# Attention with an added bias: the second q half loaded behind the bias, the bias slots one place later, and a third late-bias bank

## The chip, the core and the metric

The kernel runs on one core of a Trainium2 chip. Its time is device microseconds of one execution. Seven runs before the change gave a median of 250.71 us, between 250.09 and 253.24 us. One execution was recorded by the hardware profiler; all durations of instructions below come from it.

## The reference

Four batches of eight heads, 1024 positions, 64 values per head. One bias matrix of 1024 by 1024 is shared by all 32 heads.

```python
scores = np.matmul(q, k.transpose(0, 1, 3, 2)) / np.sqrt(64) + bias   # bias [1, 1, 1024, 1024]
attn = np.exp(scores - scores_max) / (np.sum(np.exp(scores - scores_max), axis=-1, keepdims=True) + 1e-8)
out = np.matmul(attn, v)
```

## The kernel before, in words

**Work units.** The heads are taken in 16 pairs. The scores are held transposed: keys on the 128 partitions, 512 queries along the free dimension. Such a block of 128 keys by 512 queries of one head is called a *bank*; there are 512 of them. The banks of a pair run over query half 0 first (16 banks: 8 key chunks by 2 heads) and then over query half 1. So banks 0 to 15 need only the first query half of pair 0, and bank 16 is the first that needs its second half. In the last 16 banks the order is one head after the other.

**Slots.** Banks are grouped into slots, one PSUM buffer and one exp each: slot S0 holds bank 0, S1 banks 1 and 2, and from S2 on each slot has three (S2: 3 to 5, S6: 15 to 17, S7: 18 to 20). The last two are S168 with banks 507 to 509 and S169 with banks 510 and 511. The PSUM pool `ps_s` has two buffers, so a slot can be filled only when the exp of the slot before the last has ended.

**One slot's way.** TensorE fills it (`s_fill`, L130: one matmul of kT with qT a bank). ScalarE takes the exp of it in one instruction (`s_exp`, L137) and writes bf16 to a tile E in SBUF. The bias enters as a factor: exp(score + bias) is exp(score) times exp(bias). VectorE multiplies E by `eb`, the exp of the transposed bias, two or four banks an instruction (`mul_pair`, L156, L159, L162). TensorE then multiplies E by v with a column of ones (`av_bank`, L187; for the last eight banks `av_last`, L223), and VectorE divides by the sum (L197, L199; for the last eight banks L232, L236 and L238) before the output DMA.

**The bias factor.** `eb` is made in four units. In each, 16 TensorE transposes of the raw bias `btraw` go to a PSUM buffer of the same pool `ps_s` (`b_fill`, L145), and one ScalarE exp writes 128x2048 values (`b_exp`, L150). The four units B(0,0), B(0,4), B(1,0), B(1,4) stand at fixed places in the list `order` of slots, L328 to L330.

**Late-bias banks.** For the last banks the bias is added ahead of the exp, as an extra matmul of the identity with `braw` (L133), so that no multiplication comes after the exp. `late_bias` names them (L110): banks 510 and 511. `late_bias_pe` (L164 to L175) makes `braw` from `btraw` by eight transposes and one VectorE instruction with the factor 8 (L174); the piece `(NP, 0, 0)` stands for it in the planner.

**Loads.** k and q of pair 0 come in two halves. The first halves come through the SyncE and ScalarE queues in float32. The second ones, and everything later, are issued by GpSimd with a cast to bf16. At the start GpSimd issues:

```python
nc.gpsimd.dma_start(out=kr0[:, :, QC:, :]..., in_=kf[0][:, :, QC * D:])   # L261: k, second half
nc.gpsimd.dma_start(out=qr0[:, :, QC:, :]..., in_=qf[0][:, :, QC * D:])   # L262: q, second half
nc.gpsimd.dma_start(out=btraw[:, :QC, :], in_=bf_[:, :QC, :])             # L263: bias rows of query half 0
```

After them come v of pair 0 (L81), the other half of the bias (L318), and k, q and v of the next pairs (L75, L76, L81). The second q half of pair 0 is transposed on TensorE (L89) and copied into qT with a mask on VectorE (L98). Then S6 can be filled.

**Order.** Slots S0 to S2 are written out by hand. From S3 on a planner inside the kernel, with costs of its own and due times for the loads (`bias_at`, `raw_at`), decides in which order each engine's instructions are written; each engine then runs its list in order and waits on semaphores. The planner's times decide only this order. Its table `ends` says that the last multiplications take one bank (506), two (507, 508) and one (509); `pe_last` holds banks 508 and 509 together for L223.

Of the kernel before, what the change touches and what calls it, by code (L numbers as in the profile page):

```python
# [15 lines left out]
def kernel(  # L16
# [41 lines left out]
    warm = consts.tile([P, 1], F32)  # L58
    btraw = consts.tile([P, NCH, S], BF)
    eb = consts.tile([P, 2, NCH, HQ], BF)  # L60
    braw = consts.tile([P, 2, HQ], BF)
    mask = consts.tile([P, 2, HQ], BF)
    vall = consts.tile([P, 2 * NP, NCH, D1], BF)

# [18 lines left out]
    def transpose_pe(pr, which, half, tag):  # L83

        src = raws[pr][which]
        px = ps_x.tile([P, QC, P], BF, tag=tag, name="px")
        for c in range(QC):
            for t in range(2):
                nc.tensor.transpose(px[t * D:(t + 1) * D, c, :], src[:, t, half * QC + c, :], ident[:])  # L89
        if (pr, which) not in trs:  # L90
            trs[(pr, which)] = (kvp.tile([P, NCH, P], BF, name="kT") if which else
                                kvp.tile([P, 2, NCH * P], BF, name="qT"))
        dst = trs[(pr, which)]

        def copy():
            if which == 0:

                nc.vector.tensor_tensor(dst[:, :, half * HQ:(half + 1) * HQ],  # L98
                                        px.rearrange("p c q -> p (c q)").unsqueeze(1).to_broadcast([P, 2, HQ]),
                                        mask[:], op=ALU.mult)  # L100
            else:
                nc.vector.tensor_copy(dst[:, half * QC:(half + 1) * QC, :], px[:])  # L102
        return copy
# [3 lines left out]
    NB = len(banks)  # L107

    banks[NB - 16:] = [(NP - 1, h, 1, kc) for h in range(2) for kc in range(NCH)]
    late_bias = {NB - 2: 0, NB - 1: 1}  # L110
    slots = [[0], [1, 2]] + [list(range(i, min(i + 3, NB))) for i in range(3, NB, 3)]
    NS = len(slots)
    ET = 12
# [47 lines left out]
        else:  # L161
            nc.vector.tensor_tensor(e, e, eb[:, qh, kc:kc + 1, :].to_broadcast([P, n, HQ]), op=ALU.mult)  # L162

    def late_bias_pe(tag):  # L164

        px = ps_x.tile([P, 2, HQ], BF, tag=tag, name="px")
        for j in range(2):
            for i in range(QC):
                nc.tensor.transpose(px[:, j, i * P:(i + 1) * P],
                                    btraw[:, QC + i, :].rearrange("p (kp kc) -> p kc kp", kc=NCH)[:, NCH - 2 + j, :],  # L170
                                    ident[:])

        def copy():
            nc.vector.tensor_scalar(braw[:], px[:], 1.0 / scale, None, op0=ALU.mult)  # L174
        return copy  # L175

    oalls = {}
# [64 lines left out]
    with tc.manual_schedule():  # L242
# [16 lines left out]
        nc.gpsimd.memset(qT0[D:, 0, :HQ], 0.0)  # L259
        nc.gpsimd.memset(qT0[:D, 1, :HQ], 0.0)  # L260
        nc.gpsimd.dma_start(out=kr0[:, :, QC:, :].rearrange("p t c d -> p t (c d)"), in_=kf[0][:, :, QC * D:])  # L261
        nc.gpsimd.dma_start(out=qr0[:, :, QC:, :].rearrange("p t c d -> p t (c d)"), in_=qf[0][:, :, QC * D:])  # L262
        nc.gpsimd.dma_start(out=btraw[:, :QC, :], in_=bf_[:, :QC, :])  # L263
        for x in range(2):
            for y in range(2):
                nc.vector.memset(mask[x * D:(x + 1) * D, y, :], 1.0 if x == y else 0.0)
# [59 lines left out]
        EXP, EXP0, QK, AV, TP = 427, 62, 216, 170, 350  # L326
        MUL, COPYQ, COPYK, EVAC, SEM = 600, 650, 420, 620, 80
        order = [("S", g) for g in range(3, NS)]  # L328
        for at, x in ((4, (0, 0)), (6, (0, 4)), (9, (1, 0)), (11, (1, 4))):
            order.insert(at, ("B",) + x)  # L330
        NO = len(order)
        T0 = 8000.0
# [2 lines left out]
        act_end = []  # L335
        x_free = {"xa": T0 - 500, "xb": T0 + 100}
        x_unit = {}
        bias_at = [13300, 20800]
        raw_at = {0: (5900, 7800), 1: (22200, 23500), 2: (26000, 28500)}
        pieces = [(0, 0, 1)]  # L340
        for pr in range(1, NP):
            pieces += [(pr, 1, 0), (pr, 0, 0), (pr, 1, 1), (pr, 0, 1)]

        pieces.append((NP, 0, 0))
        raw_at[NP] = (T0, T0)
        piece_end = {(0, 1, 0): T0, (0, 0, 0): T0, (0, 1, 1): T0 + 200}
        eb_at = {}
# [13 lines left out]
            return banks[b][:3]  # L361

        dve_q = []
        ends = {NB - 6: 1, NB - 5: 2, NB - 3: 1}

        def pe_cost(t, c):
            return c * 2 if t < COLD else c
# [13 lines left out]
        def pe_fill():  # L381
            i = len(filled)
            if i >= NO or i - 2 >= len(act_end):
                return None
            ready = act_end_of(i - 2) + SEM
            item = order[i]
            if item[0] == "S":
                for b in slots[item[1]]:
                    pr, h, qh, kc = banks[b]
                    for key in ((pr, 1, kc // QC), (pr, 0, qh)) + (((NP, 0, 0),) if b in late_bias else ()):  # L390
                        if key not in piece_end:
                            return None
                        ready = max(ready, piece_end[key] + SEM)
                cost = QK * (len(slots[item[1]]) + sum(b in late_bias for b in slots[item[1]]))
            else:
                ready = max(ready, bias_at[item[1]])
                cost = 2 * TP + 250

            def emit(t):
                if item[0] == "S":  # L400
                    s_fill(item[1])
                else:
                    b_fill(item[1], item[2])
                filled.append(t + pe_cost(t, cost))
            return ready, cost, emit

        def pe_piece():
            if not pieces:
                return None
            pr, which, half = pieces[0]  # L410
            if pr not in raw_at or (pr < NP and pr not in raws):
                return None
            i = min(len(filled), NO - 1)
            while order[i][0] != "S":
                i -= 1
            at = slots[order[i][1]][0]
            if at < (pr - 2) * 32 + 8:
                return None

            left = NCH - av_next % NCH  # L420
            busy = x_unit.get(unit_of(av_order[av_next])) if av_next < NA and av_next % NCH else None
            tags = sorted((x_free[x], x) for x in x_free if x != busy)
            if busy and left < 4 and at < pr * 32 - 16:
                return None
            if not busy and av_next and at < pr * 32 - 16 and tags[0][0] + SEM < t_pe and len(tags) > 1 and tags[1][0] > t_pe:
                return None
            free, tag = tags[0]
            ready = max(free + SEM, raw_at[pr][1 - which])
            cost_t = TP if pr < NP else 720

            def emit(t):
                pieces.pop(0)
                copy = transpose_pe(pr, which, half, tag) if pr < NP else late_bias_pe(tag)
                cost = COPYK if which else COPYQ
                x_free[tag] = 1e12

                def run(t2):
                    copy()
                    x_free[tag] = t2 + cost
                    piece_end[(pr, which, half)] = t2 + cost  # L440
                    if pr < NP and which == 0 and half == 1:
                        if pr + 3 < NP:
                            load_qk(pr + 3)
                            raw_at[pr + 3] = (t2 + 7000, t2 + 7000)
                        if pr + 2 < NP:
                            load_v(pr + 2)
                dve_q.append((t + pe_cost(t, cost_t) + SEM, 0, cost, run))
            return ready, cost_t, emit
# [3 lines left out]
        def pe_last():  # L452

            best = None
            for x in range(2):
                left = last_left[x]
                if not left or (x == 1 and last_tag[0] is None):
                    continue
                steps = [[b] for b in left if b not in (NB - 4, NB - 3)] or [[NB - 4, NB - 3]]
                for bs in steps:  # L460
                    if any(b not in mul_at for b in bs):
                        continue
                    ready = max(mul_at[b] for b in bs) + SEM
                    tag = last_tag[x]
                    if tag is None and x == 0:
                        free, tag = min((x_free[y], y) for y in x_free)
                        ready = max(ready, free + SEM)
                    elif tag is None:
                        if len(act_end) < NO - 1 or len(filled) < NO:
                            continue  # L470
                        tag = "s"
                        ready = max(ready, act_end[NO - 2] + SEM)
                    c = (max(ready, t_pe), x, bs, tag)
                    if best is None or c[0] < best[0]:
                        best = c
            if best is None:
                return None
            ready, x, bs, tag = best
            cost = len(bs) * AV // 2

            def emit(t):
                if last_tag[x] is None and x == 0:
                    x_free[tag] = 1e12
                last_tag[x] = tag
                evac = av_last(x, bs, tag)
                if evac:
                    dve_q.append((t + cost + SEM, 1, EVAC, lambda t2: evac()))
            return ready, cost, emit
# [152 lines left out]
```

## Time and profile before

| what | value |
|---|---|
| median of 7 runs | 250.71 us |
| the profiled execution's own time | 250.79 us |
| its span, first to last instruction | 249.0 us |
| ScalarE busy | 239.9 us (96%) |
| TensorE matmul busy | 229.1 us (92%) |
| VectorE busy | 220.7 us (89%) |
| GpSimd busy | 53.6 us (22%) |
| 172 exps of E (L137) | 230.0 us |
| 4 exps of the bias (L150) | 7.5 us |
| ScalarE in the exp of S0 | from 5.87 us |
| last exp of E ends | 243.21 us |

The busy share is read with the idle time of each engine's largest group beside it. The 172 exps have 0.4 us of idle time before them in total, and the four bias exps 0.3 us. The profiled execution's time is its span and 1.8 us around it, and it lies 0.08 us above the median.

### The profile page before, as it was taken

Reading aid. Unit: us, or ns where it says so; the run is one execution under the profiler, and the core shown is the slowest. Engines: PE = TensorE matmul, PEld = TensorE weight load, DVE = VectorE, ACT = ScalarE, POOL = GpSimd, SP = SyncE. Lnnn points to the kernel's source line nnn. Section 1 sums busy time; section 2 is a strip of 40 time slices with the busy share of each in tenths; the row PEclk is TensorE's granted clock in tenths of the full one; section 3 lists DMA queues with packets and bytes.
Section 4 is the critical chain, followed back from the end, with each engine's and each line's share of the span. In section 5 each row is a group of like instructions: output and inputs, shape, how many; then the busy total and the mean of one; then the engine's idle time right before and its main releaser. Section 6 shows DMA issues by size and latency. Waiting matters only on the chain.

```text
span 249.0 us, 7212 instructions
## 1 busy us (share of the span) xinstructions
PE 229.1 (92%) x3160; PEld 140.7 (56%) x3160; DVE 220.7 (89%) x393; ACT 239.9 (96%) x183; POOL 53.6 (22%) x74
## 2 busy tenths in 40 slices
PE   7768999999999999999999999999999999998991
PEld 4346656666555565655655665555565555565561
DVE  5236999999999999999999989999999999998882
ACT  4999999999999999999999999999999999999991
POOL 6653534104013050315050400501600000000000
PEclk9999999999999999999999999999999999999998
DMA  5999999924935649496968921582981111020211
GB/s 122 182 204 188 199 126 206 90 87 54 156 49 92 79 98 116 91 125 85 129 81 120 132 53 42 87 129 42 147 70 42 45 40 48 3 84 3 87 42 46
DMA packets 48464, 23.80 MB, mean 96 GB/s; under 512 B 34480, under 2 KB 44592, under 8 KB 48176
## 3 DMA queue, kind: packets, MB, share of 16 engines
q0 software_dynamic: 42272, 14.42, 53.5%
q1 hardware_dynamic: 5872, 8.72, 9.8%
q8 instruction: 25, 0.41, 0.6%
q10 hardware_dynamic: 288, 0.20, 0.2%
q14 instruction: 7, 0.06, 0.1%
HBM read 29.36 MB, written 8.39 MB: 152 GB/s over the span
## 4 chain that ended last, share of the span: by engine, by line
ACT 57%; PE 20%; DVE 14%; DMA 4%; issue 2%; POOL 1%; ACTq 0%; POOLq 0%
ACT E L137 54%; PE ps L130 12%; DVE E L162 5%; PE po L187 5%; DMA btraw<-in_bias_dram 4%; ACT eb L150 3%; PE px L89 2%; DVE qT L98 2%; DVE E L159 2%; DVE oall L199 2%; DVE E L156 1%; DVE rs L197 1%; DVE kT L102 1%; PE pb L145 0%; POOL kr L261 0%
## 5 line engine op out<-in xcount | busy, mean ns | idle before, releaser
L137 ACT ACTIVATE E<-ps 128x1536 bf16<-128x1536 f32 (+2 forms) x172 | 230.0, 1700 | 0.4 <-PE ps L130 0.4
L130 PE MATMUL ps<-qT,kT 128*128 128x512 bf16 x512 | 138.4, 377 | 8.5 <-ACT E L137 5.3
L187 PEld LDWEIGHTS <-E 128*128 128x128 bf16 x2016 | 81.3, 97 | 40.1 <-DVE E L162 5.1
L187 PE MATMUL po<-vall,E 128*128 128x65 bf16 x2016 | 92.5, 194 | 2.4 <-DVE E L162 1.3
L159 DVE TENSOR_TENSOR E<-E,eb 128x2048 bf16<-128x2048 bf16 x66 | 79.8, 1216 | 6.8 <-ACT eb L150 6.4
L162 DVE TENSOR_TENSOR E<-E,eb 128x1024 bf16<-128x1024 bf16 x116 | 76.6, 683 | 2.7 <-ACT E L137 1.9
L130 PEld LDWEIGHTS <-kT 128*128 128x128 bf16 x512 | 45.2, 96 | 39.7 <-issue 8.4
L75 POOL DMA_DIRECT2D kr<-in_k_dram x15 | 10.5, 700 | 90.8 <-PE px L89 85.2
L81 POOL DMA_DIRECT2D vall<-in_v_dram x32 | 28.1, 883 | 4.9 <-DVE kT L315 3.8
L199 DVE TENSOR_TENSOR oall<-po,rs 128x256 f32<-128x256 f32 x63 | 26.8, 425 | 2.2
L98 DVE TENSOR_TENSOR qT<-px,mask 128x1024 bf16<-128x1024 bf16 x31 | 21.3, 688 | 4.0 <-PE px L89 3.1
L76 POOL DMA_DIRECT2D qr<-in_q_dram x15 | 10.8, 717 | 29.5 <-PE px L89 25.5
L102 DVE COPY kT<-px 128x512 bf16<-128x512 bf16 x30 | 12.6, 421 | 1.8 <-PE px L89 1.2
L197 DVE RECIPROCAL rs<-po 128x4 f32<-128x4 f32 x63 | 11.1, 176 | 2.0 <-PE po L187 1.7
L89 PEld LDWEIGHTS <-qr 128*64 128x64 bf16 x248 | 8.0, 109 | 8.7 <-issue 5.9
L89 PE MATMUL px<-ident,qr 128*64 128x128 bf16 x248 | 12.8, 225 | 0.0
L89 PE MATMUL px<-ident,kr 128*64 128x128 bf16 x240 | 12.4, 224 | 0.1
L89 PEld LDWEIGHTS <-kr 128*64 128x64 bf16 x240 | 7.7, 109 | 7.8 <-issue 3.6
L150 ACT ACTIVATE eb<-pb 128x2048 bf16<-128x2048 bf16 x4 | 7.5, 1877 | 0.3 <-PE pb L145 0.3
L145 PE MATMUL pb<-ident,btraw 128*128 128x128 bf16 x64 | 4.7, 226 | 2.3 <-ACT eb L150 1.5
L145 PEld LDWEIGHTS <-btraw 128*128 128x128 bf16 x64 | 4.4, 147 | 3.2 <-issue 1.6
L156 DVE TENSOR_TENSOR E<-E,eb 128x1024 bf16<-128x1024 bf16 (+2 forms) x7 | 4.6, 686 | 0.2 <-ACT E L137 0.2
(44 smaller groups left out, 27.5 us busy)
## 6 DMA issues: line engine op xcount, KB each, us to landing
out_dram<-oall SPq DMA_DIRECT2D x28, 256.0 KB, 2.0
vall<-in_v_dram POOLq DMA_DIRECT2D x32, 128.0 KB, 5.6
kr<-in_k_dram POOLq DMA_DIRECT2D x15, 256.0 KB, 3.9
qr<-in_q_dram POOLq DMA_DIRECT2D x15, 256.0 KB, 5.1
btraw<-in_bias_dram POOLq DMA_DIRECT2D x2, 1024.0 KB, 9.7
out_dram<-oall SPq DMA_DIRECT2D x7, 128.0 KB, 3.8
k0f<-in_k_dram SPq DMA_DIRECT2D x2, 128.0 KB, 2.9
q0f<-in_q_dram ACTq DMA_DIRECT2D x1, 128.0 KB, 2.7
```

The source lines that it names most:

```text
L81: nc.gpsimd.dma_start(out=vall[:, 2 * pr + t, :, :D], in_=vf[pr, :, t])
L89: nc.tensor.transpose(px[t * D:(t + 1) * D, c, :], src[:, t, half * QC + c, :], ident[:])
L98: nc.vector.tensor_tensor(dst[:, :, half * HQ:(half + 1) * HQ], px.rearrange("p c q -> p (c q)").unsqueeze(1).to_broadcast([P, 2, HQ]), ma ...
L102: nc.vector.tensor_copy(dst[:, half * QC:(half + 1) * QC, :], px[:])
L130: nc.tensor.matmul(ps[:, j, :], kT[:, kc, :], qT[:, h, qh * HQ:(qh + 1) * HQ], start=True, stop=b not in late_bias)
L137: nc.scalar.activation(e_at(slots[g][0], n), open_ps.pop(("S", g))[:, :n, :], ACTF.Exp, scale=scale)
L150: nc.scalar.activation(eb[:, qh, k0:k0 + 4, :], open_ps.pop(("B", qh, k0))[:, :4, :], ACTF.Exp)
L159: nc.vector.tensor_tensor(e, e, eb[:, qh, kc:kc + 2, :].unsqueeze(2).to_broadcast([P, 2, 2, HQ]), op=ALU.mult)
L162: nc.vector.tensor_tensor(e, e, eb[:, qh, kc:kc + 1, :].to_broadcast([P, n, HQ]), op=ALU.mult)
L187: nc.tensor.matmul(acc[:, i, :], e[:, 0, i * P:(i + 1) * P], vall[:, 2 * pr + h, kc, :], start=(kc == 0 and i == 0), stop=(kc == NCH - 1), ...
L197: nc.vector.reciprocal(rs[:], acc[:, :, D:D1])
L199: nc.vector.tensor_tensor(oall[:, c0:c0 + QC, :], acc[:, :, :D], rs[:].to_broadcast([P, QC, D]), op=ALU.mult)
```

## The change

- The load of the second q half of pair 0 is issued behind the load of the first half of the bias instead of ahead of it. The planner's due times follow: the bias at 12.9 us (before 13.3) and 20.2 us (before 20.8), this q half at 13.7 us (before 7.8).
- The four bias units stand one slot later in `order`. The exps run S2 to S7, B(0,0), S8, B(0,4), S9, S10, B(1,0), S11, B(1,4); before they ran S2 to S6, B(0,0), S7, B(0,4), S8, S9, B(1,0), S10, B(1,4).
- Three banks take the bias ahead of the exp: 509, 510 and 511. `braw` has three parts, made in two pieces: one of two banks and one of one bank. Bank 509 has no multiplication after the exp any more, and `pe_last` takes 508 and 509 singly.

From the added line in `late_bias_pe` on, line numbers are one higher after the change.

```diff
-    braw = consts.tile([P, 2, HQ], BF)
+    braw = consts.tile([P, 3, HQ], BF)
...
-    late_bias = {NB - 2: 0, NB - 1: 1}
+    late_bias = {NB - 3 + i: i for i in range(3)}
...
-    def late_bias_pe(tag):
-
-        px = ps_x.tile([P, 2, HQ], BF, tag=tag, name="px")
-        for j in range(2):
+    def late_bias_pe(j0, tag):
+
+        n = min(2, 3 - j0)
+        px = ps_x.tile([P, n, HQ], BF, tag=tag, name="px")
+        for j in range(n):
             for i in range(QC):
                 nc.tensor.transpose(px[:, j, i * P:(i + 1) * P],
-                                    btraw[:, QC + i, :].rearrange("p (kp kc) -> p kc kp", kc=NCH)[:, NCH - 2 + j, :],
+                                    btraw[:, QC + i, :].rearrange("p (kp kc) -> p kc kp", kc=NCH)[:, NCH - 3 + j0 + j, :],
                                     ident[:])
         def copy():
-            nc.vector.tensor_scalar(braw[:], px[:], 1.0 / scale, None, op0=ALU.mult)
+            nc.vector.tensor_scalar(braw[:, j0:j0 + n, :], px[:], 1.0 / scale, None, op0=ALU.mult)
...
         nc.gpsimd.dma_start(out=kr0[:, :, QC:, :].rearrange("p t c d -> p t (c d)"), in_=kf[0][:, :, QC * D:])
+        nc.gpsimd.dma_start(out=btraw[:, :QC, :], in_=bf_[:, :QC, :])
         nc.gpsimd.dma_start(out=qr0[:, :, QC:, :].rearrange("p t c d -> p t (c d)"), in_=qf[0][:, :, QC * D:])
-        nc.gpsimd.dma_start(out=btraw[:, :QC, :], in_=bf_[:, :QC, :])
...
-        for at, x in ((4, (0, 0)), (6, (0, 4)), (9, (1, 0)), (11, (1, 4))):
+        for at, x in ((5, (0, 0)), (7, (0, 4)), (10, (1, 0)), (12, (1, 4))):
             order.insert(at, ("B",) + x)
...
-        bias_at = [13300, 20800]
-        raw_at = {0: (5900, 7800), 1: (22200, 23500), 2: (26000, 28500)}
+        bias_at = [12900, 20200]
+        raw_at = {0: (5900, 13700), 1: (22200, 23500), 2: (26000, 28500)}
...
-        pieces.append((NP, 0, 0))
+        pieces += [(NP, 0, j) for j in range(2)]
...
-        ends = {NB - 6: 1, NB - 5: 2, NB - 3: 1}
+        ends = {NB - 6: 1, NB - 5: 2}
...
-                steps = [[b] for b in left if b not in (NB - 4, NB - 3)] or [[NB - 4, NB - 3]]
+                steps = [[b] for b in left]
```

## The prediction

> **What bounds the kernel now.** I read the page's busy table and costliest groups first.
>
> ```profile
> PE 229.1 (92%) x3160; PEld 140.7 (56%) x3160; DVE 220.7 (89%) x393; ACT 239.9 (96%) x183; POOL 53.6 (22%) x74
> ...
> L137 ACT ACTIVATE E<-ps 128x1536 bf16<-128x1536 f32 (+2 forms) x172 | 230.0, 1700 | 0.4 <-PE ps L130 0.4
> ...
> L150 ACT ACTIVATE eb<-pb 128x2048 bf16<-128x2048 bf16 x4 | 7.5, 1877 | 0.3 <-PE pb L145 0.3
> ```
>
> ScalarE runs 176 exps from 5.87 us to 243.21 us with 0.7 us of idle time before them. Exps of three banks follow each other every 1.34 us (part of the recorded length overlaps the next). So ScalarE is the limit from end to end: a delay in front of any exp is paid in full, and a gain can only come from its small gaps, its start at 5.87 and the tail after 243.21. The other engines can give nothing in between.
>
> Next, the timeline of the first 18 us, start and length first:
>
> ```profile
> 9.87 0.41 PE L89 MATMUL px<-ident,qr 128*64 128x128 bf16 x8
> 10.33 0.69 DVE L98 TENSOR_TENSOR qT<-px,mask 128x1024 bf16<-128x1024 bf16 x1 [1.99 <-PE px L89]
> 11.82 0.81 PE L130 MATMUL ps<-qT,kT 128*128 128x512 bf16 x3 [0.54 <-ACT E L137]
> 12.97 1.49 ACT L137 ACTIVATE E<-ps 128x1536 bf16<-128x1536 f32 x1
> 13.48 1.21 PE L145 MATMUL pb<-ident,btraw 128*128 128x128 bf16 x16 [0.85 <-DMA btraw<-in_bias_dram]
> 14.72 1.88 ACT L150 ACTIVATE eb<-pb 128x2048 bf16<-128x2048 bf16 x1 [0.27 <-PE pb L145]
> 16.63 2.36 DVE L159 TENSOR_TENSOR E<-E,eb 128x2048 bf16<-128x2048 bf16 x2 [5.62 <-ACT eb L150]
> ```
>
> The second q half is transposed at 9.87 and copied to qT by 11.02. The fill at 11.82 is S6 (banks 15 to 17), the first that needs it. Its exp starts at 12.97, without a wait. The exp of B(0,0) starts 1.75 after that instead of 1.34: it waited 0.41 us for the bias. That wait is what the earlier bias load can remove.
>
> Then the loads on GpSimd's queue, by the timeline (issue), the chain of waits (the bias) and the issues of the first 9 us (size, time from issue to landing):
>
> ```profile
> 2.42 0.83 POOL L261 DMA_DIRECT2D kr<-in_k_dram  x1
> 3.25 0.73 POOL L262 DMA_DIRECT2D qr<-in_q_dram  x1
> 3.96 9.47 DMA btraw<-in_bias_dram
> ```
> ```profile
> kr<-in_k_dram POOLq DMA_DIRECT2D x1, 128.0 KB, 3.7
> qr<-in_q_dram POOLq DMA_DIRECT2D x1, 128.0 KB, 5.0
> vall<-in_v_dram POOLq DMA_DIRECT2D x1, 128.0 KB, 6.1
> ```
>
> So k lands at 2.42 + 3.7 = 6.12, q at 8.25, the bias at 3.96 + 9.47 = 13.43, and the v load issued at 8.38 at 14.48. They land in the order of issue; v, though issued five microseconds before the bias was in, came 1.05 us after it. The queue works in order, and a load put behind the 1 MB bias waits for it.
>
> Last, the tail:
>
> ```profile
> 240.56 2.65 ACT L137 ACTIVATE E<-ps 128x1536 bf16<-128x1536 f32 x2
> 241.93 1.42 DVE L156 TENSOR_TENSOR E<-E,eb 128x512 bf16<-128x512 bf16 x3
> 243.27 0.17 DVE L197 RECIPROCAL rs<-po 128x4 f32<-128x4 f32 x1
> 244.56 1.42 SPq L239 DMA_DIRECT2D out_dram<-oh  x1
> ```
>
> After the last exp, VectorE runs without a gap through the last of these three multiplications (banks 506, 507-508, 509), a division and the division of the last eight banks, to the last output DMA.
>
> **The q half behind the bias.** Its landing is the largest unknown. The three loads together carry the same bytes over the same queue, so the last of them should land when the last did before: 13.43. Lower bound: the bias takes 13.43 - 8.25 = 5.18 us behind the load ahead of it, so it could land at 6.12 + 5.18 = 11.30, and q as long after it as v did, at 12.35. Upper bound: the bias keeps its 9.47 us from its new issue at about 3.25 (12.72), and q lands 1.05 later, at 13.77. I take 13.43: q's own stretch behind k was 2.13 us, not 1.05, and the sum of bytes speaks for it.
>
> From the landing to the exp of S6: TensorE starts 0.05 after a landing (13.43 to 13.48); the mask copy starts 0.46 after the first transpose (9.87 to 10.33) and takes 0.69; a matmul follows a VectorE copy by 0.05 (kT ready at 8.34, matmul at 8.39); banks 16 and 17 take 0.60 (bank 15 doesn't wait; three take 0.81, so one step is 0.22 and the last 0.38); the exp follows 0.03 after. Sum 1.88, so the exp of S6 starts at 13.43 + 1.88 = 15.31 instead of 12.97: **+2.34 us** (1.26 to 2.68).
>
> Nothing covers this. In the built program's order TensorE has, behind the fill of S5, the eight q transposes, then S6, S7 and only then the transposes of the bias. The bias would be in before q, but it is queued behind the q transposes on TensorE and behind S6 and S7 on ScalarE. That is the step where the two edits work against each other: the slots were moved later, when the only work ready in time is the bias. VectorE's copies and multiplications queue behind the same wait.
>
> TensorE idles from 11.28, the end of S5's fill, to 13.48. The granted clock is 1.00 in every stretch up to there, and the longest idle time seen was 0.85 us, after which 16 transposes ran in the usual 1.21.
>
> The Trainium skill ("TensorE: Matmul & The Clock Gate", Part 1) says that an idle window of about 3.4 us halves the clock. These 2.2 us are shorter, so by the rule it costs nothing; did a window catch it, an estimate by the page's factor of two on the two matmuls and transposes would be about 1 us more.
>
> **The bias one slot later.** The 0.41 us in front of B(0,0) go: **-0.41**. A smaller wait comes instead. B(0,0) uses the PSUM buffer of S6, freed at 15.31 + 1.48 = 16.79; its transposes take 1.21 and end at about 18.03, while ScalarE, after S6 and S7, is free at 15.31 + 2 x 1.34 = 17.99. So some 0.05 us, and as much at the other units that follow two slots: **+0.15** in all (0 to 0.4, as tight fills before cost 0.1 or less each). S8 to S11 find their buffers in time by the same walk. The issue of the bias on GpSimd moves up by 0.73 and q's back by 0.60; nothing later on that queue moves, and no SyncE issue does.
>
> **Three late-bias banks.** Removed: the multiplication of bank 509 (0.42), whose successor would start 0.33 earlier. Added: four transposes (eight took 0.41, so 0.25) and one VectorE instruction of 128x512 (0.42, as the multiplication of that size; the L174 row of 128x1024 took 0.68). They fall near 226 us, where VectorE was busy 3.25 of the 4 us from 228 to 232 and TensorE 3.33: hidden, and 0.67 at worst without cover. One more matmul of 0.22 in the fill of S168 ends that fill 0.16 after ScalarE is ready, so its exp and the multiplication of 507-508 come 0.15 later. The last fill starts when the exp of S167 frees its buffer, at 241.00 as before, so the last exp stays. Net **-0.18** (-0.33 to 0): the chain behind it is the same divisions and DMA, and TensorE's eight last matmuls after the last exp are done by then.
>
> **Sum.** 2.34 - 0.41 + 0.15 - 0.18 = +1.90 us. On the profiled execution (250.79, with 1.8 us around the span of 249.0) that is 252.7; on the median of 250.71, 252.6. By the bounds: 1.26 - 0.41 - 0.33 = +0.5 and 2.68 - 0.41 + 0.4 = +2.7.
>
> **The rivals.**
>
> *The q half is not held up by the bias* (not slower). If the 16 DMA engines took packets of both loads in turn, or the bias stream ran faster from its earlier start, q could land early. No stall is left if it lands before 12.97 - 1.88 = 11.09; then only -0.41, +0.15 and -0.18 count: 250.3. It decides from a landing before about 12.8: then the sum is under 1.25 us. For it speaks that the lower bound lies at 12.35; against it the landings in strict order and v's 1.05 us behind the bias. Chance 0.17, of which 0.06 for no stall at all.
>
> *VectorE's late start stalls TensorE* (slower still). The first multiplication waits for B(0,0): by the walk until 18.04 + 1.88 = 19.92 instead of 16.63, 3.3 us later, while ScalarE is 2.1 later. VectorE then trails by 1.2 us more, and from 27 to 236 us it is busy 200 of 209 us, so it needs about 28 us to catch up. An E-times-v group that waits in front of a fill would hold the exps. It costs at most those 1.2 us, plus the 0.67 of the extra piece if that isn't hidden: 253.2 to 254.4. Against it: the order was planned with a late q, and E has six buffers of 12 banks. Chance 0.10.
>
> *The third late-bias bank moves the end by nothing*, because the final chain is held by TensorE or the exp: 252.8, inside the range, and part of the main case.
>
> **How the numbers follow.** Main case 0.73, 252.6 by its sum. The range goes from 251.5, leaving out the no-stall case and the lowest corner of the landing (together about 0.1), to 253.4, which takes the upper bound of the sum and leaves out most of the second rival. About 0.5%, 1.25 us, is what a measurement of this kernel can tell from no change. Slower by more: the main case, the second rival: 0.83 less a little for a landing between, 0.82. Within it: 0.17. Faster by more: the removable gaps (0.41, 0.33) don't add up to 1.25 us, 0.01.
>
> **What would show it.** In the profile after: a wait of L137 on L130 of about 2.3 us before the exp of S6, and a start near 15.3; the q transposes starting at a DMA landing near 13.4; no DMA wait in front of the transposes of the bias; L150 without its 0.27; two `braw` instructions on VectorE near 221 and 227 us and no multiplication of one bank behind 507-508; the last exp some 2.1 us later, and 5.5 us instead of 5.7 from its end to the end of the span. I am wrong if the q transposes start by 11, or if ScalarE shows the exp of S6 without a wait.

## The result and the profile after

| | before | after |
|---|---|---|
| median | 250.71 us | 252.46 us (26 runs, 250.48 to 255.03) |
| ratio after to before | | 1.0044 (1.0027 to 1.0061): +1.1 us (0.7 to 1.5) |
| the profiled execution | 250.79 us | 251.8 us |
| its span | 249.0 us | 250.0 us |

The ratio leaves out the few runs over 1.5% above the fastest of their kernel, the medians do not; so the two do not agree. A repeat on another occasion (e12 below) gave 1.0086 (1.0045 to 1.0126).

The page after: the busy table and the two exp groups.

```profile
PE 231.8 (93%) x3165; PEld 142.3 (57%) x3165; DVE 220.1 (88%) x392; ACT 240.1 (96%) x183; POOL 53.6 (21%) x74
...
L137 ACT ACTIVATE E<-ps 128x1536 bf16<-128x1536 f32 (+2 forms) x172 | 230.2, 1668 | 2.1 <-PE ps L130 2.1
...
L150 ACT ACTIVATE eb<-pb 128x2048 bf16<-128x2048 bf16 x4 | 7.5, 1879 | 0.4 <-PE pb L145 0.4
```

ScalarE does the same work, but waits 2.1 us for fills (L130) where it waited 0.4; 1.12 us of that stand in front of S6. The loads of the first microseconds (size, time from issue to landing) and the timeline show why:

```profile
btraw<-in_bias_dram POOLq DMA_DIRECT2D x1, 1024.0 KB, 8.5
...
qr<-in_q_dram POOLq DMA_DIRECT2D x1, 128.0 KB, 8.7
```
```profile
12.55 0.41 PE L89 MATMUL px<-ident,qr 128*64 128x128 bf16 x8 [0.70 <-DMA qr<-in_q_dram]
13.01 0.69 DVE L98 TENSOR_TENSOR qT<-px,mask 128x1024 bf16<-128x1024 bf16 x1 [4.11 <-PE px L89]
13.76 2.29 PE L130 MATMUL ps<-qT,kT 128*128 128x512 bf16 x5 [0.47 <-DVE qT L98]
14.80 2.79 ACT L137 ACTIVATE E<-ps 128x1536 bf16<-128x1536 f32 x2 [1.12 <-PE ps L130]
17.80 1.88 ACT L150 ACTIVATE eb<-pb 128x2048 bf16<-128x2048 bf16 x1 [0.20 <-PE pb L145]
```

The q half, issued at 3.81, lands at 12.51, 0.7 us behind the bias. TensorE waits for it, VectorE copies, the fill of S6 follows and the exp of S6 starts at 14.80 after a wait. The five matmuls at 13.76 take 2.29 us; before, three took 0.81. The windows view (TensorE's busy time first, of 3.40 us) says why: the column behind the five engines is the granted clock.

```profile
10.30:13.70 3.40, 1.76 (x13) 0.56 (x12) 0.69 (x1) 3.38 (x3) 3.40 (x6) 1.00 1.61 148
13.70:17.10 3.40, 3.09 (x13) 1.50 (x13) 0.00 (x1) 2.29 (x2) 2.89 (x4) 0.50 1.02 187
```

From 13.7 us on the clock is at half for one 3.4 us stretch. The tail (start, length):

```profile
243.33 1.62 DVE L156 TENSOR_TENSOR E<-E,eb 128x1024 bf16<-128x1024 bf16 x3
...
246.03 0.17 DVE L233 RECIPROCAL rh<-po 128x2 f32<-128x2 f32 x1 [0.33 <-PE po L224]
```
```profile
246.56 0.33 SPq L240 DMA_DIRECT2D out_dram<-oh  x1
```

VectorE is early now and waits 0.33 us for TensorE's last matmuls. SyncE's last issue takes 0.33 us where it took 1.42.

The one microsecond between the two spans splits so, from the starts of the exps: S2 begins 0.57 later (8.20, before 7.63), since the matmuls of the first three banks took 0.63 us each in this execution instead of 0.38, ahead of anything the change touches; from the start of S2 to the end of the last exp it is 236.94 us instead of 235.58, +1.36 (mainly +1.26 in front of S6, +0.31 in front of B(0,0), +0.29 in front of B(1,0), and -0.41 for the wait that went); from the end of the last exp to the end of the span it is 4.89 us instead of 5.81, -0.92. Sum +1.01.

### The profile page after: what moved, and what is told of

Its sections match the earlier page's. It is cut to its first block, busy times and chain, and to the rows that moved or that the text cites. A ratio compares the mean times of both kernels' runs of the same rounds, so it can differ in the third digit from the quotient of the medians.

```text
span 250.0 us, 7222 instructions
## 1 busy us (share of the span) xinstructions
PE 231.8 (93%) x3165; PEld 142.3 (57%) x3165; DVE 220.1 (88%) x392; ACT 240.1 (96%) x183; POOL 53.6 (21%) x74
## 4 chain that ended last, share of the span: by engine, by line
ACT 64%; DVE 14%; PE 10%; DMA 6%; issue 3%; POOL 1%; ACTq 0%
ACT E L137 63%; PE ps L130 5%; DMA kr<-in_k_dram 4%; DVE E L162 4%; DVE E L159 4%; PE po L188 2%; DVE qT L98 2%; DVE oall L200 2%; ACT eb L150 1%; DMA q0f<-in_q_dram 1%; DVE E L156 1%; PE px L89 1%; POOL vall L81 1%; DVE kT L102 1%; DVE rs L198 1%
## 5 line engine op out<-in xcount | busy, mean ns | idle before, releaser
L130 PE MATMUL ps<-qT,kT 128*128 128x512 bf16 x512 | 140.0, 381 | 8.5 <-ACT E L137 5.2
L159 DVE TENSOR_TENSOR E<-E,eb 128x2048 bf16<-128x2048 bf16 x67 | 80.8, 1216 | 6.0 <-ACT eb L150 6.0
L162 DVE TENSOR_TENSOR E<-E,eb 128x1024 bf16<-128x1024 bf16 x114 | 75.5, 683 | 2.7 <-ACT E L137 1.9
L130 PEld LDWEIGHTS <-kT 128*128 128x128 bf16 x512 | 45.4, 97 | 40.2 <-issue 9.3
L89 PE MATMUL px<-ident,qr 128*64 128x128 bf16 x248 | 12.8, 225 | 0.7 <-DMA qr<-in_q_dram 0.7
L89 PE MATMUL px<-ident,kr 128*64 128x128 bf16 x240 | 12.4, 225 | 0.3 <-DMA kr<-in_k_dram 0.2
```

The source lines that it names most:

```text
L130: nc.tensor.matmul(ps[:, j, :], kT[:, kc, :], qT[:, h, qh * HQ:(qh + 1) * HQ], start=True, stop=b not in late_bias)
L159: nc.vector.tensor_tensor(e, e, eb[:, qh, kc:kc + 2, :].unsqueeze(2).to_broadcast([P, 2, 2, HQ]), op=ALU.mult)
```

## The experiments

Theory: the q half lands when all bytes ahead of it on the queue have landed, S6 waits for it, and in the pause the clock falls. Rivals: the later slots or the third bank cost the time; or the loads as a whole became slower. "q late" below is a load behind the bias.

**e1: the q half first again, the rest as changed.**

```diff
-        nc.gpsimd.dma_start(out=btraw[:, :QC, :], ...)
         nc.gpsimd.dma_start(out=qr0[:, :, QC:, :]..., ...)
+        nc.gpsimd.dma_start(out=btraw[:, :QC, :], ...)
-        bias_at = [12900, 20200]; raw_at = {0: (5900, 13700), ...
+        bias_at = [13300, 20800]; raw_at = {0: (5900, 7800), ...
```

> The changed kernel with one part undone: the second q half is loaded ahead of the bias again (due times as before); the bias slots one place later and the third late-bias bank stay. Theory (the loss is the wait of S6 for the q half and the clock that falls in it): the exp of S6 follows S5 after 1.34 us, the exp of B(0,0) follows S7 without a wait, no matmul at half clock from 10 to 20 us; time about 0.4 to 0.6 us under the kernel before, some 250.2 us, and 1.5 to 2 us under the changed kernel. Rival (the later slots or the third bank cost the time): it stays near 252 us.

Measured: 250.67 us, ratio 0.9982 (0.9952 to 1.0011), -0.5 us. ScalarE's timeline:

```profile
9.18 6.82 ACT L137 ACTIVATE E<-ps 128x1536 bf16<-128x1536 f32 x5
15.88 1.89 ACT L150 ACTIVATE eb<-pb 128x2048 bf16<-128x2048 bf16 x1
```

The exp of S6 and that of B(0,0) do not wait, although the bias landed only at 14.41. The clock was at full speed there. So the load order is the loss. The gain expected on top is not clear of noise. The profile, of an execution of 254.07 us, shows a wait of another kind, 2.51 us in front of B(1,0), on pair 1's k; e8 below has it too, and there it is shown.

**e2: the load order alone, in the kernel before** (the same two loads swapped, and the due times).

> The kernel before with one part of the change alone: the bias loaded ahead of the second q half (with the planner's new due times); slots and late-bias banks as before. Theory: the same wait of S6 as in the changed kernel, 1.2 to 2.3 us by where q lands, then B(0,0) right behind S6, whose transposes wait for the PSUM buffer of S5 alone: 251.7 to 252.7 us. If the later slots were what costs, it would be within 0.3 us of the kernel before.

Measured: 253.64 us, ratio 1.0103 (1.0073 to 1.0133), +2.6 us (1.8 to 3.3); the median is an upper miss of the expected 251.7 to 252.7. The q half landed at 14.33, S6 started at 16.84 and the clock fell too:

```profile
14.37 0.64 PE L89 MATMUL px<-ident,qr 128*64 128x128 bf16 x8 [2.72 <-DMA qr<-in_q_dram]
...
16.84 1.45 ACT L137 ACTIVATE E<-ps 128x1536 bf16<-128x1536 f32 x1 [3.37 <-PE ps L130]
```

The swap alone costs more than the whole change did (1.0027 to 1.0061), as if the other two parts gave something back; against the repeat, 1.0045 to 1.0126, that is not shown.

**e3: the third late-bias bank alone.**

```diff
-    late_bias = {NB - 2: 0, NB - 1: 1}
+    late_bias = {NB - 3 + i: i for i in range(3)}
```
(with `braw`, `late_bias_pe`, the pieces, `ends` and `pe_last` as in the change)

> The kernel before with the third late-bias bank alone; loads and slots as before. Prediction's step: VectorE's tail is shorter by 0.18 us (0 to 0.33), so 250.5 us. Reading of the profile after: TensorE's 24 last matmuls (1.0 us) now hold the end, so the gain is 0 and the time that of the kernel before, 250.7 us.

Measured: 250.03 us, ratio 0.9971 (0.9946 to 0.9996), -0.7 us (-1.4 to -0.1). It is lower than both values expected, and the one version here whose interval lies below the kernel before. e7 and e10, the same kernel with one more small ScalarE copy, gave 0.9992 and 0.9987 with intervals that reach over 1, so the gain is 0.2 to 0.7 us and hardly clear of noise.

**e12: the changed kernel again.**

> The changed kernel once more, for a second profile. Theory: the q half lands anywhere between 12.5 and 14.4 us, as the last of the three loads did in every profile so far; the exp of S6 follows that landing by 1.9 us, or by 2.3 where the clock has fallen; median 252.2 to 252.7 us.

Measured: 253.57 us (251.31 to 254.62), a miss above. The profile:

```profile
14.29 0.64 PE L89 MATMUL px<-ident,qr 128*64 128x128 bf16 x8 [2.89 <-DMA qr<-in_q_dram]
...
15.71 2.29 PE L130 MATMUL ps<-qT,kT 128*128 128x512 bf16 x5 [0.24 <-DVE qT L98]
16.76 2.79 ACT L137 ACTIVATE E<-ps 128x1536 bf16<-128x1536 f32 x2 [3.53 <-PE ps L130]
```

The same chain, with the q half at 14.24 instead of 12.51, and a wait of 3.53 us instead of 1.12.

**e5: TensorE kept busy in the pause.**

```diff
+        if g in (3, 4, 5):
+            dz = ps_x.tile([P, HQ // 2], F32, tag="xb", name="dz")
+            for _ in range(8 if g == 5 else 4):
+                nc.tensor.matmul(dz[:], zeros[:, :P], zeros[:], start=True, stop=True)
```

> The changed kernel with idle TensorE time filled: 4, 4 and 8 matmuls of zeros (128x256, about 0.11 us each, into a PSUM tile that nothing reads) behind the fills of S3, S4 and S5. Theory (in the pause before the q half the granted clock falls, and the fill of S6, S7 and B(0,0) run at half speed): the matmuls of S6 and S7 keep 0.22 us from one to the next, and 0.5 to 0.8 us of the loss go; 251.6 to 252.0 us where the changed kernel has 252.5. Rival (the pause alone is the loss, the clock hides behind ScalarE): no change, 252.5 us.

Measured: the clock stays, the time does not move: 252.49 us, ratio 1.0046 (1.0020 to 1.0071). In the profile (its lines are four higher from there on, L141 is the exp) the same five matmuls take 1.24 us, and the clock column stays at 1.00:

```profile
13.16 0.41 PE L89 MATMUL px<-ident,qr 128*64 128x128 bf16 x8 [0.48 <-DMA qr<-in_q_dram]
...
14.37 1.24 PE L130 MATMUL ps<-qT,kT 128*128 128x512 bf16 x5 [0.47 <-DVE qT L98]
14.99 2.79 ACT L141 ACTIVATE E<-ps 128x1536 bf16<-128x1536 f32 x2 [1.35 <-PE ps L130]
```
```profile
10.30:13.70 3.40, 2.82 (x25) 1.73 (x24) 0.08 (x1) 3.34 (x3) 3.40 (x5) 1.00 1.74 174
13.70:17.10 3.40, 2.04 (x16) 1.13 (x15) 0.61 (x1) 2.11 (x2) 2.16 (x4) 1.00 1.08 214
```

S6 follows the landing (13.12) by 1.87 us, against 2.29 and 2.52 in the two profiles of the changed kernel, so the fall costs some 0.4 to 0.65 us there. That this moves the median is not shown: the interval, 1.3 us wide, and the spread of the landing are larger.

**e4: B(0,0) ahead of S6.**

```diff
-        for at, x in ((5, (0, 0)), (7, (0, 4)), (10, (1, 0)), (12, (1, 4))):
+        for at, x in ((3, (0, 0)), (5, (0, 4)), (9, (1, 0)), (11, (1, 4))):
```

> The changed kernel with the bias units at places 3, 5, 9 and 11 of the list instead of 5, 7, 10 and 12: B(0,0) stands ahead of S6. The bias, landing at 11.8 to 12.4 us, is then the work that is ready while q is not. Theory: B(0,0) waits 0 to 0.7 us for its transposes, S6 has its q by then and does not wait; TensorE has work in the former pause, so the clock stays; 250.3 to 251.0 us. Rival (the queue change itself slows all loads or the whole start): it stays near 252 us.

Measured: 252.53 us, ratio 1.0050 (1.0017 to 1.0084). The expectation is missed; the step that failed is the landing of the bias, 13.11 in this profile and not 11.8 to 12.4. TensorE paused 2.20 us for it, B(0,0) began 1.73 us late, and S6 0.52 more at half clock. Neither load was there when ScalarE was free, at 12.65. The time is the one that the rival named, slower loads as a whole; the landings below do not show such loads.

**e8: half of the bias ahead of the q half, half behind.**

```diff
-        nc.gpsimd.dma_start(out=btraw[:, :QC, :], in_=bf_[:, :QC, :])
+        nc.gpsimd.dma_start(out=btraw[:, :2, :], in_=bf_[:, :2, :])
         nc.gpsimd.dma_start(out=qr0[:, :, QC:, :]..., ...)
+        nc.gpsimd.dma_start(out=btraw[:, 2:QC, :], in_=bf_[:, 2:QC, :])
```

> The changed kernel with the first bias load cut in two loads of 512 KB, and the q half between them. Theory (the q half lands when the bytes ahead of it have landed): it lands some 2.6 us sooner, at 9.9 to 11.7, S6 waits 0 to 0.6 us and usually not at all, the bias is in time for its later slot; 250.0 to 250.6 us. Rival (the wait comes from being second behind any bias load, not from bytes): 252 us or more.

Measured: 251.56 us, ratio 1.0018 (0.9993 to 1.0042), between the two. The q half landed at 11.54, and S6 started 0.28 us late, 1.87 behind the landing at full clock. Bytes ahead, not the place behind a bias load, set the wait. The due times, which e1 and e2 changed together with the loads, are those of the changed kernel here, so they are not the cause either. The median is 1 us over what was expected, and the profile shows a wait that no step had:

```profile
22.05 0.41 PE L89 MATMUL px<-ident,kr 128*64 128x128 bf16 x8 [1.70 <-DMA kr<-in_k_dram]
...
23.51 1.45 ACT L137 ACTIVATE E<-ps 128x1536 bf16<-128x1536 f32 x1 [1.07 <-PE ps L130]
```

With the slots one later the planner set the transposes of pair 1's k ahead of the fill of S10 (in e1 ahead of B(1,0)). k landed at 22.0, TensorE stood 1.70 us in front of it, and the exps of S10 and B(1,0) waited 1.07 and 0.52 us. In the changed kernel ScalarE is late by then and the same order costs less, 0.29 us in front of B(1,0).

**e6 and e7: the two last output issues.** ScalarE and SyncE each issue one output DMA at the end, 0.04 us apart before and 0.27 us apart with a third bank. SyncE's took 1.42 us before, 1.32 in e2, and 0.33 in every profile with the third bank. The two runs ask whether that is the 0.92 us of the tail.

```diff
                 for i in range(M):
                     nc.scalar.activation(oh[:, i, :], acc[:, i, :D], ACTF.Copy, scale=rs[:, i, :])
+                lag = small.tile([P, 2, D], F32, name="lag")
+                for i in range(2):
+                    nc.scalar.activation(lag[:, i, :], acc[:, 0, :D], ACTF.Copy, scale=rs[:, 0, :])
```
(e6 on the kernel before; e7 on e3, with one copy)

> The kernel before with two more small ScalarE copies (128x64, into a tile that nothing reads) ahead of ScalarE's last output DMA, which is so issued 0.4 us later, 0.4 behind SyncE's instead of 0.04. Theory (two issues at the same moment hold each other up, which is why SyncE's last issue took 1.42 us before and 0.33 us after): SyncE's issue takes 0.33 us, the end comes about 0.6 us sooner although an engine does more; 250.1 us. Rival (SyncE's issue waits for its own queue's DMA of 0.63 us earlier): it stays at 1.3 to 1.4 us, and the time at 250.6 us or 0.1 more.

> The kernel before with the third late-bias bank alone (as e3_third_bank_alone, 250.0 us), and one more small ScalarE copy ahead of ScalarE's last output DMA, so that it is issued within 0.06 us of SyncE's. Theory (issues at the same moment hold each other up): one of the two issues takes 1.3 to 1.4 us again, and the time goes up by about 0.9 us to that of the kernel before. Rival (SyncE's own queue, whose last issue is 1.03 us earlier here): both stay at 0.33 to 0.36, the time within 0.2 us of 250.0.

Measured: 250.39 us, 0.9981 (0.9957 to 1.0004), and 250.69 us, 0.9992 (0.9965 to 1.0019). Both edits missed their aim: the output DMA waits for its own tile alone, and was issued at the same moment as without the copies (1.39 and 1.15 us after the last exp). They tell nothing on the question, except that SyncE's issue took 1.10 us in e6 and 0.33 in e7 again.

**e9 and e10: the same with the copies in the tile that the DMA reads.**

```diff
-                for i in range(M):
+                for i in list(range(M)) * 2:              # e9, on the kernel before
+                for i in list(range(M)) + [M - 1]:        # e10, on e3
                     nc.scalar.activation(oh[:, i, :], acc[:, i, :D], ACTF.Copy, scale=rs[:, i, :])
```

> The kernel before with ScalarE's two last copies written twice into the tile that its output DMA reads, so that this DMA has to wait for them and is issued some 0.4 us later (in e6_act_issue_late_before the added copies went to another tile, the DMA did not wait for them and was issued at the same moment as SyncE's). Theory (two issues within 0.04 us hold each other up): SyncE's last issue takes 0.33 us instead of 1.1 to 1.4, and the end comes 0.3 to 0.8 us sooner. Rival (SyncE's issue is slow because its queue issued 0.63 us before): it stays over 1 us.

> The third late-bias bank alone, with ScalarE's last copy written twice into the tile that its output DMA reads, so that this DMA is issued 0.2 us later, within 0.06 us of SyncE's. Theory: the second of the two issues takes 1.1 to 1.4 us and the time goes up by 0.5 to 1.0 us, to about 250.8 where the third bank alone has 250.0. Rival (SyncE's own queue decides, 1.03 us since its last issue): both issues stay at 0.33 to 0.36 us.

Measured: 251.04 us, 0.9989 (0.9969 to 1.0009), and 250.86 us, 0.9987 (0.9962 to 1.0013). The issues in e9, SyncE's queue and then ScalarE's:

```profile
245.24 0.33 SPq L202 DMA_DIRECT2D out_dram<-oall  x1
245.87 0.33 SPq L239 DMA_DIRECT2D out_dram<-oh  x1
```
```profile
246.32 0.36 ACTq L239 DMA_DIRECT2D out_dram<-oh  x1
```

With ScalarE's issue 0.45 us behind, SyncE's takes 0.33, with its own queue's last issue 0.63 us earlier as before: the rival falls. But in e10 the two issues stand 0.07 us apart and neither is long, so nearness alone does not do it either. In e9's one profile, the long issue goes when ScalarE's is moved away. Whether it needs 0.04 us, or nearness and the recent issue together, stays open. Neither run's time shows the gain, and their profiles agree with that: the DMA landed 2.79 us (e9) and 2.77 us (e10) after its issue began, against 2.66 in the kernel before and 1.61 in the changed one.

**e11: the transposes of pair 1's k put later.**

```diff
-        raw_at = {..., 1: (22200, 23500), 2: (26000, 28500)}
+        raw_at = {..., 1: (24600, 25600), 2: (27200, 28500)}      # on e1
```

> The kernel of e1_q_first (q half first, bias slots one later, third bank) with the planner's due times of pairs 1 and 2 moved from 22.2 and 23.5, 26.0 and 28.5 to 24.6 and 25.6, 27.2 and 28.5 us, so that the transposes of pair 1's k stand behind the transposes of B(1,0) on TensorE and not ahead of them. Theory (the later slots bring these transposes ahead of a fill, and a k load that lands at 22 to 23.5 us then holds the exps by up to 2.6 us): no wait of S9 to B(1,0) on this load; the time falls below e1_q_first (250.7) and e3_third_bank_alone (250.0), to 249.5 us, with fewer runs over 251. Rival (the later slots bring nothing): 250.0 us.

Measured: 255.31 us, ratio 1.0178 (1.0144 to 1.0212), a miss by almost 6 us. The planner moved more than the transposes: 44 E-times-v matmuls and the transposes of both halves of k and one of q came to stand ahead of the fill of S11, and the q transposes waited 2.61 us for VectorE's copy of k, which stood behind two multiplications that waited for B(1,0). ScalarE waited 5.05 us for S11. The wait on k was gone, so that half of the expectation holds, but the version is worse than all others and does not test it cleanly.

## Why the prediction was right, point by point

**The main step holds.** The q half is held by the bytes ahead of it and S6 waits in full: undone (e1) the loss goes, alone (e2) it is there, with half the bytes (e8) most of it goes. The first rival, an early q half, never left S6 without a wait behind the whole bias. But by the prediction's own words it decides from a landing before about 12.8, and in the first profile of the changed kernel the landing, 12.51, lies there; one of five does. The argument of the sum of bytes was the right one, and the loads as a whole did not become slower: the last of the three first loads landed at 13.66 us on average in the eight profiles with q first (13.43, 14.41, 13.63, 13.43, 13.47, 14.20, 13.23, 13.46) and at 13.69 in the five with q behind the whole bias (12.51, 14.33, 14.24, 13.12, 14.24). Predicted: 13.43. What failed is its upper bound, 13.77: it came from one execution, and three of five lay above it. The lower one, 12.35, held.

**From landing to exp** the sum of 1.88 us was 1.87 in e5 and e8, and 2.29 to 2.52 where the clock had fallen.

**The clock** was costed at nothing; this step failed. The bound "the longest idle time seen was 0.85" was the wrong row: the share of busy time counts. In the changed kernel the stretch ahead of the fall has TensorE busy 1.76 of 3.40 us with no single pause over 0.75, and the clock halves; in e5 the same stretch has 2.82, and it stays. The traces give more. In each of the fourteen profiles the changes of the granted clock lie whole multiples of 3.41 us apart (here 6.85, 13.68 and 17.09; in e12 6.06, 12.89 and 19.72), so windows of that length can be laid over the execution. The 20 windows right before a fall have TensorE's matmuls busy 1.80 us or less (1.80 here, 1.38 in e12, 0.81 in e2); of those at full clock with no fall behind them, all have 1.94 or more but one, with 1.71 in e8. So the border is about half a window, and where the windows lie in an execution decides too. In the kernel before, those from 8.23 and 11.65 us have 2.35 and 2.39. Its order alone does not protect it: in e9, which has it, the bias landed at 14.20, the window from 11.28 has 1.25, and the clock fell at 14.69. The Trainium skill ("TensorE: Matmul & The Clock Gate", Part 1) speaks of an idle window of about 3.4 us and of windows that run free; the length of the halved stretch agrees, but a half-busy window was enough here.

**The bias one slot later.** The 0.41 us went, as said, but 0.31 us (after) and 0.59 us (e12) came back in front of B(0,0), since its transposes wait for S6 and run in the slow stretch; +0.15 was too small. "S8 to S11 find their buffers in time" overlooked what stands between them: the transposes of pair 1's k, which the shifted order puts ahead of a fill (e8).

**The third late-bias bank.** (The last slots, numbered S167 to S169 above, are S169 to S171: there are 172, counted from 0.) -0.18 us was predicted from VectorE. VectorE did come early, but TensorE's last matmuls took its place, as the third rival had it: SyncE's issue starts 1.42 us after the last exp, before 1.35. The -0.92 us of the profile lies behind that, between the start of this issue and its landing (1.61 us instead of 2.66), which the sum did not contain. That the shorter issue makes it is not shown: in e9, e10 and e1 the issue was as short and the landing came 2.77 to 3.16 us after its start. From run to run the last landing adds up to 1.6 us of its own: with the third bank it came 3.0 us after the last exp in six profiles and 3.9 to 4.6 in four, without it 3.7 to 4.3 in four. So the -0.92 is in part the draw of one execution, and its cause stays open.

**The sum** of +1.90 us stands against +1.1 (0.7 to 1.5) and, in the repeat, +2.2 (1.1 to 3.2); 252.6 against a median of 252.46. The size was met partly by luck: in the first profile the clock, costed at nothing (0.4 to 0.65 us), and the tail, 0.74 us shorter than predicted, offset each other, and the landing lay 0.92 us ahead of the one in the sum. "Slower by over 0.5%" is not settled by the first interval, 0.27 to 0.61%; the repeat's lies almost all above it. The second rival, VectorE's late start stalling TensorE, left no trace: after 27 us the profile shows no idle time in front of any exp, in either kernel.

## What to carry to other kernels

On this queue the first loads landed in the order of issue in all fourteen profiles. There, putting a small load behind a large one costs the small one the large one's whole time (the q half landed at 12.5 to 14.3 us instead of 8.0 to 9.1), and the gain of the large one is only what the small one took (the bias landed at 12.92 us on average instead of 13.66). Ask which of the two the next instruction in the fixed order needs first, and move its consumer together with it. A landing read from one profile is one draw: before building on it, compare it with other executions, and give the bound the spread. A planner's due time is not a local edit: one changed number reordered everything behind it (e11).

## What the hardware showed that was not expected

- The granted clock fell to 0.50 after windows of 3.41 us in which TensorE was busy about half the time or less, in the changed kernel without a pause over 0.75 us; 16 short matmuls of zeros in the gaps kept it at 1.00. It came back after one such window in which TensorE was busy 2.73 us or more; with 2.59 (e2) and 1.77 us (e12) it stayed down for a second one, 6.83 us in all.
- The last of the first loads on GpSimd's queue ends anywhere between 12.5 and 14.4 us in executions of nearly the same program. In part a few of the sixteen completions come late: in e2 fourteen of the bias's had landed by 11.95 and two at 13.5 and 13.7; in e9 and e12 two came over 1.1 us behind the rest, in e4 six.
- SyncE's last DMA issue took 1.10 to 1.42 us in the three profiles in which ScalarE's began 0.04 to 0.05 us later, and 0.33 us in all others; the time from its start to the landing was 1.6 us in six profiles and 2.3 to 3.2 us in eight, and did not follow the length of the issue.
